# The values of differential attention made for two heads at a time, with x as the weights

## The chip, the cores and the metric

The kernel runs on one core of one Trainium2 chip. The metric is the device time of one execution in microseconds (us): lower is better. The engines are named as the profile names them: PE is TensorE (PEld its weight loads), DVE is VectorE, ACT is ScalarE, POOL is GpSimd, SP is the engine that issues the DMAs.

## What is computed

One step of a hybrid streaming encoder layer over 384 tokens: 256 of a prompt, and 16 new tokens of each of 8 sequences that have a cache of 128 earlier tokens. x has 2048 columns. One projection of x feeds two branches, differential attention (8 heads) and a gated delta rule (16 heads, "GDN" below). Their outputs are merged through gates, and a norm, cross attention and a feed-forward network follow. The part that matters here:

```python
def diff_attention_block(q, k, v, q_pos, k_pos, lam):
    s = jnp.einsum("bqhmd,bkhmd->bhmqk", q, k).astype(jnp.float32) * (DIFF_HEAD_DIM ** -0.5)
    ...
    p = jax.nn.softmax(jnp.where(allowed, s + bias, -jnp.inf), axis=-1)
    wts = p[:, :, 0] - lam * p[:, :, 1]
    return jnp.einsum("bhqk,bkhe->bqhe", wts.astype(v.dtype), v)
    ...
    proj = jnp.einsum("btd,de->bte", x, w_in)
    dq, dk, dv, gq, gk, gv, gz, ga, gb, gate_a, gate_b = split_in(proj)
    qd = dq.reshape(B, T, N_DIFF_HEADS, 2, DIFF_HEAD_DIM)
    kd = dk.reshape(B, T, N_DIFF_HEADS, 2, DIFF_HEAD_DIM)
    vd = dv.reshape(B, T, N_DIFF_HEADS, DIFF_VDIM)
    ...
    o_a = (rms_norm(o_a, diff_subln_g) * (1.0 - lam_init)).reshape(B, T, DIFF_WIDTH)
```

The keys and values of the new tokens are outputs of the kernel too (`dk`, `dv`).

## The kernel before

**Matrix jobs.** Every large product is a `Job` in one list that `stream` (line 400) works through. x and the weights are split in a high and a low part (`xh`, `xl`; `wh`, `wl`), and each product takes three fp32r matmuls: high by high, and twice high by low. Weights arrive in halves of 512 KB (8 tiles of 128 x 128) through four `raw` buffers. `prep` (line 376) casts a half to `wh` on ACT and subtracts on DVE to make `wl`; three pairs of such buffers run ahead of PE. There are two forms of job:

- `job` (line 341) uses the weights as the stationary operand and streams x's 384 tokens: 16 steps of 3 matmuls, 128 x 384, into one PSUM accumulator `acc`. The result has output channels on its partitions.
- `jobt` (line 358) uses tiles of 128 tokens of x as the stationary operand and streams 512 weight columns: 16 steps of 3 token tiles of 3 matmuls, 128 x 512, into three accumulators. The result has tokens on its partitions. Before the change it makes the cross attention's values from the memory (`memh`, `meml`), and the products of w_o (`mixh`), w_xo (`xoh`) and w_ff2 (`fh`).

The pool `psm` has three accumulators. A job's accumulator is emptied by a task of its own (`evac`).

**Attention.** `diff_jobs` (line 1163) makes for each head six such jobs of 128 channels: two of q, two of k, two of v. `begin` stands after head 0's six jobs; it closes the GDN branch and opens the attention's pools. From there `lane` takes the heads one after the other through `diff_head` (line 1266), a generator that runs between the matrix jobs. It first transposes v, 128 x 128 at a time, three into each of two PSUM tiles `dtr`, and ACT copies them to `vt`. Then come three query tiles: 0 (128 keys), 1 (256 keys), 2 (the new tokens, with the cache `kc`, `vc`). Each tile is one chain over the engines:

PE scores `dsc` -> DVE bias, maximum, scale (`dtt`, `dst`) -> ACT two exponentials with their sums -> DVE quotient and difference (`dtt`) -> PE transposes `dtr` -> ACT copy `dwT` (tile 2: DVE `dwz` too) -> PE product with the values `do` -> ACT squares `dsq` -> DVE `df` -> POOL power `df` -> ACT scaling `don` -> PE transposes into `do` -> DVE `doT`.

**Order.** The order on each engine is written out when the program is built. `Driver` keeps a rough clock for each engine. After each step of a job `poll` lets those tasks go on whose inputs are ready by that clock, so that a chain's next PE piece stands behind as many matrix matmuls as its wait seems to need. `until` is called where the stream must not go on before an event: it lets tasks run until the event is set, and no matrix matmul of a later job is issued meanwhile. On PE the attention's pieces and the matrix matmuls thus stand in one fixed row.

One such place is the start of a head's first q job (`job(h, 0, 0)`, `start`, line 1224): `if h > 1: d.until(done_ev[h - 2])`, so the q job of head h stands behind the whole of head h - 2. After the last head's jobs come 6 gate jobs, and then `merge_jobs` waits for the end of the attention (`opened`, line 1387).

Nearly all instructions are issued through one helper (`call`, line 117), and the profile gives them its line 118: they are told apart by their tiles.

Of the kernel before, what the change touches and what calls it, by code (L numbers as in the profile page):

```python
# [9 lines left out]
F32 = mybir.dt.float32  # L10
# [7 lines left out]
P = 128  # L18
D = 2048
KT = 16  # L20
# [302 lines left out]
class Kern:  # L323
# [33 lines left out]

    def jobt(self, w, lhs, nt, done, begin=None, ns=KT, mid=None, second=False, apart=0):


        halves = [(w, 8 * a, 8) for a in range(ns // 2)]
        if apart:
            halves = halves[:-apart] + [x + (i,) for i, x in enumerate(halves[-apart:])]
        cut = ns - 2 * apart
        order = [(k, t) for k in range(cut) for t in range(nt)] + [(k, t) for t in range(nt) for k in range(cut, ns)]
        quanta = [((k // 2, (k % 2, t), t, k, k == 0, k == ns - 1), lhs) for k, t in order]
        return Job(halves, quanta, nt, begin, done, GW, mid, second)
# [32 lines left out]
    def stream(self, jobs):  # L400
# [8 lines left out]
        for j in jobs:  # L409
# [5 lines left out]
            if not started:  # L415
                started = True
                d.spawn(self.prep(), prio=-1, lim=1e9)
            accs = []
            freed = freeds[j.second]
            for _ in range(j.nacc):  # L420
                if len(freed) >= 3:
                    d.until(freed[-3])
                freed.append(Ev())
                t = (self.psm2 if j.second else self.psm).tile([P, 512], F32, name="acc")
                accs.append(t[:, :j.n])
            last = {q[0]: i for i, (q, _) in enumerate(j.quanta)}
            for qi, ((hf, slot, ai, k, start, stop), rhs) in enumerate(j.quanta):
# [5 lines left out]
                if r[2] is not None:  # L433
                    d.until(r[2])
                d.until(h[:, 0:8], l[:, 0:8], r[0], r[1])
                acc = accs[ai]
                if isinstance(slot, tuple):
# [12 lines left out]
                if stop:  # L450
                    freed[len(freed) - j.nacc + ai] = j.done(ai, acc)
                d.poll()
# [710 lines left out]
    def diff_jobs(self):  # L1163
# [8 lines left out]
        self.b_ev = [Ev() for _ in range(KT)]  # L1172
        v_ev = [Ev() for _ in range(NDH)]
        done_ev = [Ev() for _ in range(NDH)]
# [21 lines left out]
        def lane():  # L1196
# [15 lines left out]
            for h in range(NDH):  # L1212
                heads[h]["kc"] = kc = s["at"].tile([P, 2, BS, P], F32, name="kc", bufs=1)
                d.sync.dma_start(out=kc, in_=I["cache_k"][h])
                heads[h]["vc"] = vc = s["at"].tile([P, BS, 256], F32, name="vc", bufs=1)
                d.sync.dma_start(out=vc, in_=I["cache_v"][h])
                yield tuple(evs[h, i] for i in range(6))
                yield from self.diff_head(h, heads[h], s, v_ev[h])
                done_ev[h].set()

        def job(h, i, m):
            e = evs[h, 2 * i + m] = Ev()

            def start():
                hd = heads[h]
                if i == 0 and m == 0:
                    if h > 1:
                        d.until(done_ev[h - 2])
                    if h == 0:
                        s["at0"] = d.pool(self.bctx, "at0", side="right")  # L1230
                    pool = s["at"] if h else s["at0"]
                    hd["q"] = pool.tile([P, 2, T], F32, name="dq")
                    hd["k"] = pool.tile([P, 2, T], F32, name="dk")
                    if h == 2:
# [4 lines left out]
                if i == 2 and m == 0:  # L1239
                    if h:  # L1240
                        d.until(v_ev[h - 1])
                    hd["v"] = s["at"].tile([P, 2, T], F32, name="dv", bufs=1) if h else s["at0"].tile([P, 2, T], F32, name="dv")

            def evac(acc):
                yield acc
                dst = heads[h]["qkv"[i]]
                d.scalar.copy(dst[:, m], acc)
                yield dst[:, m]
                if i:
                    d.sync.dma_start(out=self.O["dk" if i == 1 else "dv"][h * 2 + m], in_=dst[:, m])  # L1250
                e.set()

            return self.job(I["w_diff"][h * 6 + i * 2 + m], self.rx, lambda ai, acc: self.evl.spawn(evac(acc)), start)
# [12 lines left out]
    def diff_head(self, h, hd, s, v_ev):  # L1266
        nc, c = self.d, self.c
# [6 lines left out]
        for m in range(2):  # L1274
            sv = q[:, m, TP:].rearrange("p (g e t) -> p g e t", e=2, t=TS)
            dv = qz[m].rearrange("p (g e) (f t) -> p g e f t", e=2, t=TS)
            for e in range(2):
                nc.gpsimd.tensor_copy(dv[:, :, e, e], sv[:, :, e])
        vt = at.tile([P, 3, 256], F32, name="vt")
        for e in range(2):  # L1280
            ps = pstr.tile([P, 512], F32, name="dtr")
            yield ps[:], v[:, e]
            for t in range(3):
                nc.tensor.transpose(ps[:, t * P:(t + 1) * P], v[:, e, t * P:(t + 1) * P], ident)
            yield ps[:, 2 * P:T]
            nc.scalar.copy(vt[:, :, e * P:(e + 1) * P], ps[:, :T].rearrange("p (t d) -> p t d", d=P))
        v_ev.set()
        oT = at.tile([P, 2, T], F32, name="doT", bufs=1)
        for tile_ in (0, 1, 2):
# [40 lines left out]
            if tile_ < 2:  # L1330
                nc.scalar.copy(wT[:, :nk // P], ps[:, :nk].rearrange("p (j q) -> p j q", q=P))
                yield wT[:], o[:]
                for j in range(nk // P):
                    nc.tensor.matmul(o[:, :256], lhsT=wT[:, j], rhs=vt[:, j], start=(j == 0), stop=(j == nk // P - 1))
            else:
# [6 lines left out]
                yield wT[:], o[:], wzt[:], vc[:]  # L1342
                nc.tensor.matmul(o[:, :256], lhsT=wT[:, 1], rhs=vt[:, 2], start=True, stop=False)
                for e in range(2):
# [603 lines left out]
def pack(inp):  # L1948
# [35 lines left out]
    r["w_gate"] = np.concatenate([tiles(sec["gta"]), tiles(sec["gtb"])], axis=0)  # L1984
    hd = [tiles(sec[n]).reshape(NDH, 2, P, KT, P) for n in ("dq", "dk", "dv")]
    r["w_diff"] = np.stack(hd, axis=1).reshape(NDH * 6, P, KT, P)
    for nm in ("w_pa", "w_pb", "w_xq", "w_ff1", "w_ff3"):
        r[nm] = tiles(a[nm][0])
    wide = lambda w: w.reshape(-1, P, NG, GW).transpose(2, 1, 0, 3).reshape(NG, P, -1, P)
    r["w_o"] = wide(a["w_o"][0])  # L1990
    r["w_xo"] = wide(a["w_xo"][0])
# [19 lines left out]
    "dk": (2 * NDH, P, T),  # L2011
    "dv": (2 * NDH, P, T),
    "conv_p": (P, 48, 3),
# [8 lines left out]
def unpack(o):  # L2022
    c = np.ascontiguousarray
    y = o["y"].reshape(T, D)
    kv = [o[n].transpose(2, 0, 1).reshape(T, NDH, 256) for n in ("dk", "dv")]
    mem = [o["mk"].transpose(2, 0, 1).reshape(1, 1, NMEM, NXH, P), o["mv"].reshape(1, 1, NMEM, NXH, P)]
# [28 lines left out]
```

## Time and profile before

| | before |
|---|---|
| median of 3 runs (lowest, highest) | 3134.7 us (3133.63, 3136.52) |
| the profiled execution | 3136.02 us, of which 3133.8 us is the span of the trace |
| mean granted clock of TensorE | 0.989 |
| busy share of the span | PE 98%, PEld 93%, DVE 53%, ACT 37%, POOL 12% |
| HBM read, written | 450.78 MB, 38.50 MB |

The span is the time from the first to the last instruction; the execution has 2.2 us around it. Matmuls are pipelined and their ends are modelled, so what a matmul costs PE is the distance from its start to the next one's, not its own length. The attention occupies PE from 992 us to 1453 us.

### The profile page before, as it was taken

How to read it: one execution, taken by the hardware profiler on the slowest of the kernel's cores; microseconds unless marked ns; L12 is line 12 of the kernel's file. 1: busy time of each engine (PE TensorE's matmuls, PEld its weight loads, DVE VectorE, ACT ScalarE, POOL GpSimd, SP SyncE). 2: the span in 40 equal slices, each digit the busy share in tenths (PEclk: the TensorE clock that was granted, in tenths of full speed). 3: DMA queues.
4: the chain of work that ended last, by engine and by line, in shares of the span. 5: the costliest groups of instructions: out<-in, count | busy, mean ns of one | idle time of the engine just before them, and what ended most of it. 6: DMA issues, size and time to landing. Idle time of an engine off the chain costs nothing.

```text
span 3133.8 us, 46783 instructions
## 1 busy us (share of the span) xinstructions
PE 3069.3 (98%) x18059; PEld 2922.6 (93%) x18059; DVE 1661.9 (53%) x3470; ACT 1173.0 (37%) x2046; POOL 386.1 (12%) x638
## 2 busy tenths in 40 slices
PE   9999999999998999999999998899999999999997
PEld 8999999999998999999999777699999889999986
DVE  5476887788863444434344557843333333333335
ACT  5555555554432443333223224333322223223222
POOL 0344333443200000000000010000000000000001
PEclk9999999999999999999999998899999999999999
DMA  8455455554454564455444765333333433333443
GB/s 287 138 159 151 153 156 167 158 175 144 151 178 163 167 203 164 158 188 183 153 150 148 261 224 213 106 124 128 128 126 127 131 128 128 125 126 126 155 129 106
DMA packets 188640, 492.36 MB, mean 157 GB/s; under 512 B 42480, under 2 KB 78848, under 8 KB 183552
## 3 DMA queue, kind: packets, MB, share of 16 engines
q1 hardware_dynamic: 188416, 489.37, 47.4%
q8 instruction: 141, 2.31, 0.3%
q14 instruction: 83, 0.68, 0.1%
HBM read 450.78 MB, written 38.50 MB: 156 GB/s over the span
## 4 chain that ended last, share of the span: by engine, by line
PE 96%; DVE 2%; DMA 1%; issue 0%; ACT 0%; POOL 0%; SPq 0%; DVEq 0%; ACTq 0%
PE acc L118 90%; PE ch L118 1%; PE ps L118 1%; DVE R L118 1%; PE do L118 1%; PE o L118 1%; PE dsc L118 1%; PE fb L118 1%; DMA rawx<-in_memT 0%; PE dtr L118 0%; DVE hl L118 0%; DMA raw<-in_w_xo 0%; DMA xmk<-scr_mk 0%; PE xsp L118 0%; PE xss L118 0%
## 5 line engine op out<-in xcount | busy, mean ns | idle before, releaser
L118 DVE TENSOR_TENSOR wl<-raw,wh 128x1024 fp32r<-128x1024 f32 (+1 forms) x679 | 833.2, 1227 | 1016.9 <-ACT wh L118 1010.1
L118 ACT CAST wh<-raw 128x1024 fp32r<-128x1024 f32 (+1 forms) x679 | 711.9, 1049 | 1606.8 <-PE acc L118 1365.6
L118 PE MATMUL acc<-xh,wh 128*128 128x384 f32 x2320 | 817.2, 352 | 0.0
L118 PE MATMUL acc<-xh,wl 128*128 128x384 f32 x2320 | 779.8, 336 | 0.0
L118 PE MATMUL acc<-xl,wh 128*128 128x384 f32 x2320 | 778.6, 336 | 0.0
L118 PE MATMUL acc<-hl,wh 128*128 128x384 f32 x1472 | 494.9, 336 | 7.8 <-DVE hl L118 7.4
L118 PE MATMUL acc<-hh,wh 128*128 128x384 f32 x1472 | 497.1, 338 | 0.5 <-ACT hh L118 0.5
L118 PE MATMUL acc<-hh,wl 128*128 128x384 f32 x1472 | 493.8, 335 | 0.0
L118 PEld LDWEIGHTS acc<-xh,wh 128*128 128x128 f32 x2320 | 437.7, 189 | 9.9 <-issue 8.1
L118 PEld LDWEIGHTS acc<-xl,wh 128*128 128x128 f32 x2320 | 438.1, 189 | 1.5
L118 PEld LDWEIGHTS acc<-xh,wl 128*128 128x128 f32 x2320 | 436.7, 188 | 0.0
L118 PEld LDWEIGHTS acc<-hl,wh 128*128 128x128 f32 x1472 | 277.7, 189 | 11.1 <-DVE hl L118 10.8
L118 PEld LDWEIGHTS acc<-hh,wh 128*128 128x128 f32 x1472 | 277.7, 189 | 1.9 <-ACT hh L118 1.1
L118 PEld LDWEIGHTS acc<-hh,wl 128*128 128x128 f32 x1472 | 277.5, 189 | 0.0
L118 PE MATMUL acc<-wh,fl 128*128 128x512 f32 x498 | 194.0, 389 | 0.0
L118 PE MATMUL acc<-wl,fh 128*128 128x512 f32 x498 | 193.9, 389 | 0.0
L118 PE MATMUL acc<-wh,fh 128*128 128x512 f32 x498 | 193.9, 389 | 0.0
L118 POOL TENSOR_TENSOR cy<-cy,tap 128x408 f32<-128x408 f32 x144 | 174.1, 1209 | 67.8 <-ACT tap L118 58.1
L118 DVE SCALAR_TENSOR_TENSOR sol_u<-sol_mb,sol_u 128x31 f32<-128x31 f32 (+30 forms) x864 | 167.5, 269 | 0.0
L118 POOL TENSOR_TENSOR ln_mv<-ln_mv,mhalf 128x1 f32<-128x1 f32 x9 | 5.2, 581 | 1110.2 <-DVE ln_mv L118 1110.2
L118 PEld LDWEIGHTS acc<-wl,fh 128*128 128x128 f32 x498 | 93.5, 188 | 19.5
L118 PEld LDWEIGHTS acc<-wh,fl 128*128 128x128 f32 x498 | 93.5, 188 | 19.3
(288 smaller groups left out, 3608.7 us busy)
## 6 DMA issues: line engine op xcount, KB each, us to landing
raw<-in_w_ff SPq DMA_DIRECT2D x264, 512.0 KB
raw<-in_w_gdn SPq DMA_DIRECT2D x128, 512.0 KB
raw<-in_w_diff SPq DMA_DIRECT2D x96, 512.0 KB
raw<-in_w_gate SPq DMA_DIRECT2D x64, 512.0 KB
raw<-in_w_pb SPq DMA_DIRECT2D x32, 512.0 KB
raw<-in_w_pa SPq DMA_DIRECT2D x32, 512.0 KB
raw<-in_w_o SPq DMA_DIRECT2D x32, 512.0 KB
sol_ma<-scr_ma SPq DMA_DIRECT2D x8, 1024.0 KB
```

Source lines behind the costliest of these rows:

```text
L118: r = f(*a, **k)
```

## The change

v is no longer made per head with channels on the partitions. `vjob(p)`, a `jobt`, makes the values of heads 2p and 2p + 1 together: 3 token tiles, 512 columns. The weights are packed anew (`w_dv`), `diff_head` reads `v[:, j]` in place of `vt[:, j]`, and its six transposes and two copies are gone. The output `dv` is written by token tile.

The jobs' order is now: q and k of head 0; q of head 1; `begin`; values of heads 0 and 1; k of head 1; q and k of head 2; values of heads 2 and 3; q and k of head 3; q and k of head 4; values of heads 4 and 5; and so on. The wait on `done_ev[h - 2]` at the start of a head's first q job is as it was, and the values' job of pair p > 1 waits for head 2p - 3. `lane` starts a head when its q and k and all three tiles of its values are there. In `stream` an accumulator is now taken when its first matmul is issued, and `late` puts the third token tile's first two steps behind the others' first two.

```diff
-    def jobt(self, w, lhs, nt, done, begin=None, ns=KT, mid=None, second=False, apart=0):
+    def jobt(self, w, lhs, nt, done, begin=None, ns=KT, mid=None, second=False, apart=0, late=False):
...
+        if late:
+            order[:6] = [(0, 0), (0, 1), (1, 0), (1, 1), (0, 2), (1, 2)]
...
-            accs = []
+            accs, at = {}, {}
             freed = freeds[j.second]
-            for _ in range(j.nacc):
-                if len(freed) >= 3:
-                    d.until(freed[-3])
-                freed.append(Ev())
-                t = (self.psm2 if j.second else self.psm).tile([P, 512], F32, name="acc")
-                accs.append(t[:, :j.n])
...
+                if start:
+                    if len(freed) >= 3:
+                        d.until(freed[-3])
+                    at[ai] = len(freed)
+                    freed.append(Ev())
+                    accs[ai] = (self.psm2 if j.second else self.psm).tile([P, 512], F32, name="acc")[:, :j.n]
...
-                yield tuple(evs[h, i] for i in range(6))
-                yield from self.diff_head(h, heads[h], s, v_ev[h])
+                yield tuple(evs[h, i] for i in range(4)) + tuple(dv_ev[h // 2])
+                yield from self.diff_head(h, heads[h], s)
                 done_ev[h].set()
...
+        def vjob(p):
+            def start():
+                if p > 1:
+                    d.until(done_ev[2 * p - 3])
+                v = s["at"].tile([P, 3, GW], F32, name="dv")
+                for e in range(2):
+                    heads[2 * p + e]["v"] = v[:, :, 256 * e:256 * e + 256]
+                s["v", p] = v
...
+            def evac(t, acc):
+                yield acc
+                v = s["v", p][:, t]
+                d.scalar.copy(v, acc)
+                yield v
+                d.sync.dma_start(out=self.O["dv"][t][:, p * GW:(p + 1) * GW], in_=v)
...
+            return self.jobt(I["w_dv"][p], self.rx, 3, done, start, late=True)
 
         for h in range(NDH):
             if h == 1:
+                jobs.append(job(1, 0, 0))
+                jobs.append(job(1, 0, 1))
                 jobs.append(begin)
-            for i in range(3):
+                jobs.append(vjob(0))
+            for i in range(1 if h == 1 else 0, 2):
                 for m in range(2):
                     jobs.append(job(h, i, m))
+            if h and h % 2 == 0:
+                jobs.append(vjob(h // 2))
...
-        vt = at.tile([P, 3, 256], F32, name="vt")
-        for e in range(2):
-            ps = pstr.tile([P, 512], F32, name="dtr")
-            yield ps[:], v[:, e]
-            for t in range(3):
-                nc.tensor.transpose(ps[:, t * P:(t + 1) * P], v[:, e, t * P:(t + 1) * P], ident)
-            yield ps[:, 2 * P:T]
-            nc.scalar.copy(vt[:, :, e * P:(e + 1) * P], ps[:, :T].rearrange("p (t d) -> p t d", d=P))
-        v_ev.set()
...
-                    nc.tensor.matmul(o[:, :256], lhsT=wT[:, j], rhs=vt[:, j], start=(j == 0), stop=(j == nk // P - 1))
+                    nc.tensor.matmul(o[:, :256], lhsT=wT[:, j], rhs=v[:, j], start=(j == 0), stop=(j == nk // P - 1))
```

Three places show what becomes of the row of instructions on PE. The first is the start of the attention, right after `begin`: the difference of the two programs there (- before, + after). `acc` with 384 columns is a matrix job of the old form, with 512 columns one of the new, and `dtr<-cst_all,dv` are the transposes of v.

```order
 L118 MATMUL o_11462<-cst_all,y_11464 128x128 x3
-L118 MATMUL acc<-xh,wh 128x384
-L118 MATMUL acc<-xl,wh 128x384
-L118 MATMUL acc<-xh,wl 128x384
...
+L118 MATMUL acc<-wh,xh 128x512
+L118 MATMUL acc<-wl,xh 128x512
+L118 MATMUL acc<-wh,xl 128x512
...
 L118 MATMUL dtr<-lam,cst_all 128x2
...
-L118 MATMUL dtr<-cst_all,dv 128x128 x3
```

Head 0's work now stands behind the 144 matmuls of the first values' job, and its six transposes of v have gone.

The second place is the end of head 0's tile 1 and its whole tile 2 on PE. Before, each piece is followed by matrix matmuls: these are the rows from the last piece of tile 1 to the scores of tile 2 (`dqz` is the queries' layout for the cache), after which 36 `acc` matmuls stand.

```order
L118 MATMUL do<-cst_all,don 128x128 x2
L118 MATMUL acc<-xh,wh 128x384
L118 MATMUL acc<-xl,wh 128x384
L118 MATMUL acc<-xh,wl 128x384
L118 MATMUL dsc<-dk,dq 128x128 x2
L118 MATMUL dsc<-kc,dqz_11704 32x128 x8
L118 MATMUL dsc<-kc,dqz_11705 32x128 x8
L118 MATMUL acc<-xh,wh 128x384
```

In the change, six `acc` matmuls after the scores of tile 1, the rows are these:

```order
L118 MATMUL dtr<-cst_all,dtt 128x128 x2
L118 MATMUL do<-dv,dwT 128x256 x2
L118 MATMUL do<-cst_all,don 128x128 x2
L118 MATMUL dsc<-dk,dq_11058 128x128 x2
L118 MATMUL dsc<-kc,dqz_11702 32x128 x8
L118 MATMUL dsc<-kc,dqz_11703 32x128 x8
L118 MATMUL dtr<-cst_all,dtt 128x128 x2
L118 MATMUL do<-dv,dwT 128x256
L118 MATMUL do<-vc,dwz_11704 32x256 x8
L118 MATMUL do<-cst_all,don 128x128 x2
L118 MATMUL acc<-xh,wh 128x384
```

From the transposes of tile 1 to the end of tile 2 no matrix matmul stands between the pieces. The last row is the first of head 2's first q job. In heads 2 and 4 the end of tile 2, from its `dtr` to its last `do`, has the same gap-free form in front of the q jobs of heads 4 and 6, after 24 and 27 `acc` matmuls behind the scores; their other pieces are spread as before, and so are those of the odd heads and of head 6.

The third place is the end of the last head on PE, in the change:

```order
L118 MATMUL do<-dv,dwT 128x256
L118 MATMUL do<-vc,dwz_11705 32x256 x8
L118 MATMUL acc<-xh,wh 128x384
L118 MATMUL acc<-xl,wh 128x384
L118 MATMUL acc<-xh,wl 128x384
L118 MATMUL do<-cst_all,don 128x128 x2
L118 MATMUL acc<-bh,wh 128x384
```

Before, 24 `acc` matmuls stood between the product with the cached values and the last transposes; now 3 do, and the merge's first job (`bh`) follows at once.

## Rows read from the trace of the kernel before

**Rows 1.** The page's chain that ended last, over the whole span, by engine.

```profile
PE 96%; DVE 2%; DMA 1%; issue 0%; ACT 0%; POOL 0%; SPq 0%; DVEq 0%; ACTq 0%
```

**Rows 2.** That chain in one attention stretch: start us, us, engine, tile, count.

```profile
1141.23 0.86 PE do L118 x4
...
1147.02 1.45 PE dsc L118 x36
...
1154.94 0.22 PE dtr L118 x2
...
1157.27 1.43 PE do L118 x18
...
1163.61 0.22 PE do L118 x2
...
1170.62 0.33 PE dtr L118 x3
...
1190.21 0.86 PE dsc L118 x4
1191.07 6.25 PE acc L118 x36
```

**Rows 3.** Groups of PE instructions by shape: count | busy us, mean ns.

```profile
L118 PE MATMUL acc<-wl,mixh 128*128 128x512 f32 x192 | 75.9, 396 | 0.0
...
L118 PE MATMUL acc<-wl,memh 128*128 128x512 f32 x32 | 12.5, 390 | 0.0
...
L118 PE MATMUL dtr<-cst_all,dv 128*128 128x128 f32 x48 | 8.2, 282 | 0.0
```

**Rows 4.** Timeline, the first and last of 37 consecutive 512-column matmuls: start us, us.

```profile
2419.71 0.39 PE L118 MATMUL acc<-wl,fh 128*128 128x512 f32 x1
...
2427.87 0.39 PE L118 MATMUL acc<-wl,fh 128*128 128x512 f32 x1
```

**Rows 5.** Timeline of head 7's tile 1, its own instructions without the covering ones.

```profile
1421.62 1.03 PE L118 MATMUL dsc<-dk,dq 128*128 128x256 f32 x4
...
1425.91 0.48 DVE L118 SCALAR_TENSOR_TENSOR dtt<-dtt,dst 128x256 f32<-128x256 f32 x1
...
1428.73 0.38 PE L118 MATMUL dtr<-cst_all,dtt 128*128 128x128 f32 x2
...
1429.15 0.37 ACT L118 COPY dwT<-dtr 128x256 f32<-128x256 f32 x1 [0.47 <-PE dtr L118]
...
1430.54 1.02 PE L118 MATMUL do<-vt,dwT 128*128 128x256 f32 x4
...
1431.66 0.38 ACT L118 ACTIVATE dsq<-do 128x256 f32<-128x256 f32 x1 [2.14 <-PE do L118]
...
1432.40 0.54 POOL L118 TENSOR_TENSOR df<-df,mhalf 128x1 f32<-128x1 f32 x1 [16.18 <-DVE df L118]
...
1432.52 1.05 ACT L118 CAST wh<-raw 128x1024 fp32r<-128x1024 f32 x1 [0.39 <-ACT dsq L118]
...
1433.48 0.47 ACT L118 ACTIVATE don<-do,df 128x256 f32<-128x256 f32 x1
```

**Rows 6.** Timeline of head 6's tile 2, from the product with the values.

```profile
1388.68 0.59 PE L118 MATMUL do<-vt,dwT 128*128 128x256 f32 x2
...
1390.40 0.38 ACT L118 ACTIVATE dsq<-do 128x256 f32<-128x256 f32 x1 [3.36 <-PE do L118]
```

**Rows 7.** Timeline of PE where it waits for VectorE before head 0.

```profile
992.24 0.56 PE L118 MATMUL dtr<-lam,cst_all 128*128 128x2 f32 x2 [3.05 <-DVE lam L118]
```

**Rows 8.** Stretches: us, busy of five engines, PEclk, DMA share, GB/s.

```profile
982.00:988.00 6.00, 2.33 (x11) 1.94 (x10) 2.01 (x5) 0.88 (x6) 0.85 (x1) 0.69 0.48 153
...
995.00:998.00 3.00, 3.00 (x12) 3.00 (x11) 0.00 (x0) 0.48 (x1) 0.00 (x0) 0.51 1.01 410
998.00:1001.00 3.00, 3.00 (x20) 2.96 (x19) 0.89 (x1) 1.43 (x2) 0.00 (x0) 1.00 0.38 158
```

**Rows 9.** The same view, the stretch right after the attention.

```profile
1450.00:1500.00 50.00, 50.00 (x291) 49.97 (x290) 24.36 (x26) 19.59 (x23) 0.00 (x0) 1.00 0.69 224
```

More of the change, by code (lines that the diff above doesn't have):

```diff
@@ L450, in stream @@
                 if stop:
-                    freed[len(freed) - j.nacc + ai] = j.done(ai, acc)
+                    freed[at[ai]] = j.done(ai, acc)
                 d.poll()
@@ L1172, in diff_jobs @@
         self.b_ev = [Ev() for _ in range(KT)]
-        v_ev = [Ev() for _ in range(NDH)]
+        dv_ev = [[Ev() for _ in range(3)] for _ in range(NDH // 2)]
         done_ev = [Ev() for _ in range(NDH)]
@@ L1230, in start @@
                         s["at0"] = d.pool(self.bctx, "at0", side="right")
[L1231 to L1234, printed above, removed]
+                    hd["q"] = (s["at"] if h > 1 else s["at0"]).tile([P, 2, T], F32, name="dq%d" % (h == 1))
+                if i == 1 and m == 0:
+                    hd["k"] = (s["at"] if h else s["at0"]).tile([P, 2, T], F32, name="dk")
+                if h == 2 and i == 0 and m == 0:
                         def load():
@@ L1238, in start @@
                         ends.append(d.spawn(load(), prio=6))
[L1239 to L1242, printed above, removed]
             def evac(acc):
                 yield acc
-                dst = heads[h]["qkv"[i]]
+                dst = heads[h]["qk"[i]]
                 d.scalar.copy(dst[:, m], acc)
@@ L1249, in evac, with done @@
                 if i:
-                    d.sync.dma_start(out=self.O["dk" if i == 1 else "dv"][h * 2 + m], in_=dst[:, m])
+                    d.sync.dma_start(out=self.O["dk"][h * 2 + m], in_=dst[:, m])
                 e.set()
-            return self.job(I["w_diff"][h * 6 + i * 2 + m], self.rx, lambda ai, acc: self.evl.spawn(evac(acc)), start)
+            return self.job(I["w_diff"][h * 4 + i * 2 + m], self.rx, lambda ai, acc: self.evl.spawn(evac(acc)), start)
+        def vjob(p):
[6 more added lines that the diff above has]
+                s["v", p] = v
+            def done(t, acc):
+                return self.evl.spawn(evac(t, acc))
+            def evac(t, acc):
[4 more added lines that the diff above has]
+                d.sync.dma_start(out=self.O["dv"][t][:, p * GW:(p + 1) * GW], in_=v)
+                for e in range(2):
+                    x = heads[2 * p + e]["v"][:, t]
+                    d.ready[d.key(x)] = d.due(v)
+                dv_ev[p][t].set()
+            return self.jobt(I["w_dv"][p], self.rx, 3, done, start, late=True)
         for h in range(NDH):
             if h == 1:
+                jobs.append(job(1, 0, 0))
+                jobs.append(job(1, 0, 1))
                 jobs.append(begin)
-            for i in range(3):
+                jobs.append(vjob(0))
+            for i in range(1 if h == 1 else 0, 2):
                 for m in range(2):
                     jobs.append(job(h, i, m))
+            if h and h % 2 == 0:
+                jobs.append(vjob(h // 2))
         jobs += [self.gate_job(n) for n in self.gates]
@@ L1264, in diff_jobs, with diff_head @@
         return jobs
-    def diff_head(self, h, hd, s, v_ev):
+    def diff_head(self, h, hd, s):
         nc, c = self.d, self.c
@@ L1342, in diff_head @@
                 yield wT[:], o[:], wzt[:], vc[:]
-                nc.tensor.matmul(o[:, :256], lhsT=wT[:, 1], rhs=vt[:, 2], start=True, stop=False)
+                nc.tensor.matmul(o[:, :256], lhsT=wT[:, 1], rhs=v[:, 2], start=True, stop=False)
                 for e in range(2):
@@ L1984, in pack @@
     r["w_gate"] = np.concatenate([tiles(sec["gta"]), tiles(sec["gtb"])], axis=0)
-    hd = [tiles(sec[n]).reshape(NDH, 2, P, KT, P) for n in ("dq", "dk", "dv")]
-    r["w_diff"] = np.stack(hd, axis=1).reshape(NDH * 6, P, KT, P)
+    hd = [tiles(sec[n]).reshape(NDH, 2, P, KT, P) for n in ("dq", "dk")]
+    r["w_diff"] = np.stack(hd, axis=1).reshape(NDH * 4, P, KT, P)
     for nm in ("w_pa", "w_pb", "w_xq", "w_ff1", "w_ff3"):
@@ L2011 @@
     "dk": (2 * NDH, P, T),
-    "dv": (2 * NDH, P, T),
+    "dv": (3, P, D),
     "conv_p": (P, 48, 3),
@@ L2024, in unpack @@
     y = o["y"].reshape(T, D)
-    kv = [o[n].transpose(2, 0, 1).reshape(T, NDH, 256) for n in ("dk", "dv")]
+    kv = [o["dk"].transpose(2, 0, 1).reshape(T, NDH, 256), o["dv"].reshape(T, NDH, 256)]
     mem = [o["mk"].transpose(2, 0, 1).reshape(1, 1, NMEM, NXH, P), o["mv"].reshape(1, 1, NMEM, NXH, P)]
```

1 line of the change is left out of this document (added).

## The prediction

> **What bounds the kernel now.** I read the page's chain first: over the whole span 96% of it is PE [rows 1], so PE sets the time, and any other engine counts only where PE waits for it. Then the same chain inside the attention, in order of time. It goes from `acc` to an attention piece and back to `acc` with no wait between them: 36 matrix matmuls of 384 columns take 6.25 us, 0.1736 us each, and each attention piece shows what it costs PE while it is covered, 0.22 us for a pair of transposes up to 1.45 us for the scores of tile 2 [rows 2]. In this stretch PE is full; the chains of the attention over DVE, ACT and POOL are long but hidden, since enough matrix matmuls stand between their pieces. Last I read the timeline of two heads for the length of these chains without their cover [rows 5, 6]. So what PE no longer does is worth its price on PE, and what PE now waits for costs in full. Right after the attention PE is busy in all of 50 us at the full clock [rows 9]: there is no slack later that could take a loss back.
>
> **Gain 1, transposes.** 48 transposes of v go [rows 3], in 16 groups of three. A group costs PE 0.33 us [rows 2]: 16 x 0.33 = 5.3 us. Their 16 ACT copies and their waits go too; ACT does not bound here, so these are worth nothing by themselves, and neither are the 16 copies of v out of PSUM that become 12 longer ones. The DMAs of `dv` carry the same bytes in 12 issues for 16; none waits on the path.
>
> **Gain 2, the form of the job.** Per pair of heads v took 4 jobs of 48 matmuls: 192 x 0.1736 = 33.3 us. Now it takes 144 matmuls of 512 columns. The columns are the same (73728), so only the fixed part of each matmul can be saved. 37 matmuls of that form in the feed-forward part start over 8.16 us, 0.2267 us apart [rows 4]: 144 x 0.2267 = 32.6 us, a gain of 0.7 us a pair, 2.8 us in all. The bound on the other side: with `mixh` as weights one lasts 396 ns, with `memh` 390 [rows 3]; if x behaved like `mixh`, 0.2267 + 0.006 would give 33.5 us and turn 2.8 us of gain into 0.7 of loss. I take the first: in the program's memory map the tiles of x, `memh` and `fh` begin 32 bytes past a multiple of 128, and `mixh` 96 past one. That is all I find that tells the two groups apart, so both prices stay in the range. The Trainium skill ("TensorE: Matmul & The Clock Gate", section "Back-to-back issue gap") gives N/2.4 + 2.5 ns between matmuls: 162.5 and 215.8 ns, from which I would estimate a gain of only 0.5 us over the four pairs. The rows show a fixed part of some 13 ns in place of 2.5, and the measurement decides.
>
> The third accumulator of a values' job starts four steps late, about 2.7 us (12 x 0.2267), which covers the emptying of the job before it; at the job's end the first accumulator is complete six matmuls (1.4 us) ahead of the last. I cost both hand-overs at nothing; if that cover failed, it would be about 1 us of ACT cast [rows 5] a pair.
>
> **Loss 1, head 0.** The lane is no faster than before, but it starts later: head 0 must now wait for the whole first values' job, and only the two k jobs of head 1 (96 matmuls, 16.7 us) stand between that and the first q job of head 2, which the program puts behind the end of head 0. Before, the six jobs of head 1 (288 matmuls) stood in that place. The row of PE shows the result: after the scores of tile 1 only 6 matrix matmuls, then nothing but pieces of tiles 1 and 2. PE works in its row's order, so it idles through both chains.
>
> Tile 1 from its scores to the scaled output, from rows 5: scores to difference 1421.62 to 1426.39, 4.77 us; transposes to the end of the copy 1428.73 to 1429.52, 0.79; product to the end of the power 1430.54 to 1432.94, 2.40; scaling 0.47 (there held back by a weight cast, which does not stand there now). Three hand-overs to PE that the covered trace does not show I estimate at 0.2 us each (0.1 to 0.3). Sum 9.0 us. Tile 2: its scores cost PE 0.59 us more (1.45 for 0.86, rows 2), so 5.4 to the difference; 0.79; product to squares 1388.68 to 1390.40, 1.72 [rows 6]; squares to power 1.28 and scaling 0.47 as in tile 1; 0.6 for hand-overs: 10.3 us. With the last transposes of both (2 x 0.22) it is 19.7 us. Of this PE was to spend anyway 1.04 us (6 matmuls) and 5.5 us for the pieces (0.86 + 0.22 + 0.86 + 0.22 + 1.45 + 0.22 + 1.43 + 0.22, rows 2). Lost: 13.2 us.
>
> **Loss 2, heads 2 and 4.** Heads 4 and 6 wait for them in the same way, but there the four jobs of an odd head (192 matmuls) stand between, and only the end of tile 2 is bare: 0.79 + 0.2 + 1.72 + 1.28 + 0.47 + 0.2 + 0.22 = 4.9 us from `dtr` on, less 1.87 us of PE's own pieces, 3.0 us each. Head 2's chain has a weight subtraction and a split of the GDN's output on DVE in its way, so I add 0.5: 6.5 us for both. Head 6 has no q job behind it, and the odd heads are done long before theirs.
>
> **Loss 3, head 7.** Its last transposes stand 3 matrix matmuls behind the product for 24 before. On ACT a weight cast (1.05 us) and a gate's output stand ahead of the scaling, so 1.72 us to the squares, then some 2.5 to the scaled output and 0.2: 4.4 us, less 1.4 of the product and 0.5 of the three matmuls: 2.5 us.
>
> **Loss 4, the clock.** When GDN's end leaves PE little to do, busy 2.33 of 6 us, the granted clock falls to a mean of 0.69; dense matmuls go on from 992.2 us, run at half rate at 995 to 998 (0.51), and get 1.00 again from 998 [rows 7, 8]. That is 5 us of dense work at half rate, 2.5 us lost. Head 0's bare stretch is like it: 5.5 us of work in some 19. I add 2.5 us; the ends are 0 (the clock holds) and 4 (PE's own pieces inside the chain slow down too). The skill's same page (section "The HAM clock gate") says that the half rate is the default and activity releases it; rows 8 agree in both directions.
>
> **Sum.** -5.3 - 2.8 + 13.2 + 6.5 + 2.5 + 2.5 = +16.6 us. The profiled execution took 3136.0 us, 1.3 us over the median of 3134.7, so the new median is 3134.7 + 16.6 = 3151.3, rounded to 3151 us, 0.5% slower.
>
> **Rivals.** *PE does not wait.* If matmuls behind a waiting piece were run ahead of it, losses 1 to 4 would vanish: 3134.7 - 8.1 = 3126.6 us, faster by 0.26%. It decides from the point where more than 1.8 us of the 24.7 remain. Against it: PE stood still for 3.05 us at a `dtr` that waited for DVE though matrix matmuls stood behind it [rows 7]. The skill's page (section "What happens when you issue a matmul") says that only weight loads are pulled ahead and matmuls keep their order; row 7 agrees. 5%. *About no change (up to 3141).* The chains may be hidden better than the row suggests, if the bare chain is much shorter than its covered rows: at half of losses 1 to 3 and no loss of clock it is 3134.7 - 8.1 + 11.1 = 3137.7 us. For it: in the covered rows engines are shared with weight casts; against it: I took the pieces' own lengths already. 8%. *The clock stays low for longer*, and x as weights goes at the price of `mixh`. Four bare stretches could each cost 2.5 us as head 0's does, +7.5, and the form +3.5: 3162 us. For it: the 0.69 of rows 8 came with PE still busy for more than a third of the time; against it: three of the stretches are short, some 3 us of idleness. 17%. The forecast has the remaining 70%.
>
> **The numbers.** The forecast's own range is 3145 to 3158: hand-overs 1.2 either way, clock 0 to 4, the DVE work in heads 2 and 4. The range goes to 3143 below, toward the second rival, and 3161 above, toward the third. 0.2% (6.3 us) is about what a measurement of this kernel can tell from no change: faster 5%, same 8%, slower 87%.
>
> **What would show it.** In the new profile the groups `dtr<-cst_all,dv` and `vt` are gone and 576 matmuls `acc<-w..,x..` of 512 columns start some 0.227 us apart at 1.00. PE should show two bare tiles, together some 13 us idle, at the end of head 1's k jobs, some 50 us after the first values' job begins, with waits of DVE and ACT on `dsc` and `do` in the same stretch, and PEclk below 1.00 there or just behind; two waits of about 3 us, two heads apart; and one at the end of the gates. I would be wrong if PE's idle time in the attention stayed under 10 us, if x as weights cost over 0.23 us a matmul, or if the weights' buffers ran dry behind the stall: two halves (8 us) are ready there by the order of ACT and DVE.

## The result, and the profile after

| | before | changed |
|---|---|---|
| median (lowest, highest) | 3134.28 us (3133.63, 3136.52), 4 runs | 3156.7 us (3154.18, 3158.11), 4 runs |
| the profiled execution, its span | 3136.02, 3133.8 us | 3154.18, 3152.4 us |
| mean granted clock | 0.989 | 0.986 |

The changed kernel is slower: ratio 1.007, 95% interval 1.0056 to 1.0083, +22.4 us by the medians; the forecast was +16.6 us (3151, range 3143 to 3161). The whole loss is in the attention. From the first matrix matmul behind `dtr<-lam` to the first of the merge (`acc<-bh`) PE's row takes 485.6 us for 464.7, 20.9 more; what lies ahead of it and behind it took 1.2 and 1.1 us less. (The two profiled executions differ by 18.2 us only: before's lies 1.7 us over its median, the changed one's 2.5 under.) The page's chain is of little help here: followed back from the end it reaches 985 us and no further, and its shares are of the whole span:

```profile
PE 64%; DVE 2%; issue 1%; DMA 1%; ACT 0%; POOL 0%; SPq 0%; DVEq 0%; ACTq 0%; POOLq 0%
```

So I read stretches.

The stretches of the changed kernel, in the columns of [rows 8] (us, busy of PE, PEld, DVE, ACT and POOL, PEclk, DMA share, GB/s): the attention, the stretch right behind it, and six pieces of head 0's end.

```profile
992.00:1477.00 485.00, 464.39 (x2736) 423.17 (x2735) 195.84 (x346) 176.72 (x348) 20.23 (x57) 0.97 0.49 165
1480.00:1530.00 50.00, 50.00 (x290) 50.00 (x289) 25.22 (x26) 18.74 (x20) 0.00 (x0) 1.00 0.68 223
...
1042.00:1046.00 4.00, 1.42 (x8) 1.06 (x6) 3.01 (x6) 2.42 (x6) 0.00 (x0) 1.00 0.29 91
1046.00:1050.00 4.00, 2.73 (x6) 1.47 (x6) 0.75 (x3) 0.37 (x1) 0.00 (x0) 0.57 0.57 180
1050.00:1054.00 4.00, 2.04 (x19) 1.78 (x22) 0.58 (x2) 0.95 (x3) 0.55 (x1) 0.50 0.00 0
1054.00:1058.00 4.00, 1.37 (x28) 0.85 (x20) 1.54 (x3) 0.92 (x4) 0.00 (x0) 0.50 0.00 0
1058.00:1062.00 4.00, 2.35 (x12) 1.10 (x16) 1.35 (x6) 0.44 (x3) 0.00 (x0) 0.50 0.00 0
1062.00:1066.00 4.00, 2.03 (x21) 0.92 (x14) 0.24 (x2) 0.95 (x3) 1.25 (x5) 0.80 0.00 0
```

PE is idle for 20.6 of 485 us in the attention. Before, the same view shows 0.24 us of 461:

```profile
992.00:1453.00 461.00, 460.76 (x2956) 446.68 (x2957) 194.10 (x346) 179.93 (x366) 25.18 (x60) 0.99 0.50 171
```

The stretch behind it is as full as [rows 9], so nothing is given back. At head 0's end PE is busy for half of 24 us, and most of that half at the low clock level. The groups of PE show whose waits these are (busy us, mean ns | idle time before them, and what ended it); the group `dtr<-cst_all,dv` of [rows 3] is gone.

```profile
L118 PE MATMUL acc<-wh,xh 128*128 128x512 f32 x192 | 77.0, 401 | 0.0
L118 PE MATMUL do<-dv,dwT 128*128 128x256 f32 x64 | 19.6, 410 | 3.4 <-ACT dwT L118 3.4
L118 PE MATMUL do<-cst_all,don 128*128 128x128 f32 x48 | 10.0, 291 | 9.6 <-ACT don L118 9.6
L118 PE MATMUL dtr<-cst_all,dtt 128*128 128x128 f32 x40 | 8.8, 288 | 7.3 <-DVE dtt L118 3.9 <-DVE df L118 3.4
```

The chain through head 0's tiles 1 and 2 (start us, us, engine, tile, count). It is PE's own pieces and the waits between them, from the scores of tile 1 to the next matrix matmul:

```profile
1041.49 0.86 PE dsc L118 x4
1042.36 0.90 PE acc L118 x5
...
1043.28 1.04 ACT wh L118
1044.32 0.38 ACT dk L118
1044.70 1.00 ACT dtt L118 x4
...
1046.81 0.68 PE dtr L118 x2
...
1047.93 2.09 PE do L118 x4
...
1051.96 0.69 PE do L118 x2
1052.65 2.76 PE dsc L118 x36
...
1059.30 0.68 PE dtr L118 x2
...
1060.31 3.13 PE do L118 x18
...
1065.37 0.44 PE do L118 x2
1065.81 6.79 PE acc L118 x39
```

24.3 us from 1041.49 to 1065.81. The pieces from 1046.8 to 1063.4 take about twice their price in [rows 2], or more: 2.76 us for the scores of tile 2 where they took 1.45, 3.13 for the product where it took 1.43. The matrix matmuls behind it run at full speed at once (39 in 6.79 us).

Heads 2 and 4 have their bare ends too. Head 2's pieces on PE (timeline), with what ACT did ahead of the copy `dwT`, and the stretch right behind them:

```profile
1177.53 1.04 ACT L118 CAST wh<-raw 128x1024 fp32r<-128x1024 f32 x1 [1.46 <-issue]
1177.54 0.41 PE L118 MATMUL dtr<-cst_all,dtt 128*128 128x128 f32 x2
...
1178.48 0.47 ACT L118 COPY dk<-acc 128x384 f32<-128x384 f32 x1
...
1178.85 0.27 ACT L118 COPY dwT<-dtr 128x128 f32<-128x128 f32 x1
...
1179.17 0.70 PE L118 MATMUL do<-dv,dwT 128*128 128x256 f32 x2 [1.22 <-ACT dwT L118]
...
1180.02 1.07 PE L118 MATMUL do<-vc,dwz 128*32 128x256 f32 x16
...
1183.06 0.69 PE L118 MATMUL do<-cst_all,don 128*128 128x128 f32 x2 [1.97 <-ACT don L118]
```

```profile
1180.00:1183.00 3.00, 1.07 (x16) 0.42 (x16) 0.93 (x4) 1.46 (x4) 1.04 (x5) 1.00 0.58 156
1183.00:1186.00 3.00, 2.94 (x10) 2.94 (x11) 0.42 (x1) 0.14 (x2) 0.20 (x2) 0.51 0.70 257
1186.00:1189.00 3.00, 3.00 (x17) 3.00 (x17) 0.56 (x1) 0.38 (x1) 0.00 (x0) 0.92 1.04 308
```

The bare end lasts 6.2 us, from 1177.54 to the matrix matmul at 1183.75, and is over when the clock falls: 10 matmuls where the next stretch of that length has 17. Head 4 repeats it at 1296.67 to 1302.75. The chain shows the first matrix matmuls behind either end, 39 for the 39 behind head 0:

```profile
1183.75 8.11 PE acc L118 x39
...
1302.75 8.31 PE acc L118 x39
```

### The profile page after: what moved, and what is told of

It is laid out like the page before. It is cut to its first block, busy times and chain, and to the rows that moved or that the text cites. A ratio compares the mean times of both kernels' runs of the same rounds, so it can differ in the third digit from the quotient of the medians.

```text
span 3152.4 us, 46279 instructions
## 1 busy us (share of the span) xinstructions
PE 3069.6 (97%) x17819; PEld 2894.7 (92%) x17819; DVE 1661.0 (53%) x3470; ACT 1168.3 (37%) x2026; POOL 379.8 (12%) x638
## 4 chain that ended last, share of the span: by engine, by line
PE 64%; DVE 2%; issue 1%; DMA 1%; ACT 0%; POOL 0%; SPq 0%; DVEq 0%; ACTq 0%; POOLq 0%
PE acc L118 61%; PE do L118 1%; DVE R L118 1%; PE dsc L118 1%; PE fb L118 1%; DMA xmk<-scr_mk 0%; DVE hl L118 0%; PE xsp L118 0%; PE xss L118 0%; DMA raw<-in_w_xo 0%; DVE lu L118 0%; DVE fS L118 0%; PE dtr L118 0%; DVE ln_mv L118 0%; DVE wl L118 0%
## 5 line engine op out<-in xcount | busy, mean ns | idle before, releaser
L118 PE MATMUL acc<-xh,wh 128*128 128x384 f32 x2064 | 726.9, 352 | 0.0
L118 PE MATMUL acc<-xh,wl 128*128 128x384 f32 x2064 | 693.0, 336 | 0.0
L118 PE MATMUL acc<-xl,wh 128*128 128x384 f32 x2064 | 692.0, 335 | 0.0
L118 PEld LDWEIGHTS acc<-xh,wh 128*128 128x128 f32 x2064 | 389.4, 189 | 7.4 <-issue 5.4
L118 PEld LDWEIGHTS acc<-xl,wh 128*128 128x128 f32 x2064 | 389.7, 189 | 1.6
L118 PEld LDWEIGHTS acc<-xh,wl 128*128 128x128 f32 x2064 | 388.4, 188 | 0.0
L118 PEld LDWEIGHTS acc<-hl,wh 128*128 128x128 f32 x1472 | 277.0, 188 | 11.0 <-DVE hl L118 10.7
L118 PEld LDWEIGHTS acc<-wh,fh 128*128 128x128 f32 x498 | 93.5, 188 | 19.5
```

The lines of the kernel that those rows point to most:

```text
L118: r = f(*a, **k)
```

## The experiments

The theory (A below): the change's own work is cheaper on PE, and all that it loses is bare chains, in which PE waits for the lane of heads. The rivals put part of the loss or gain elsewhere. Ratios are to runs of the kernel before on the same chip (3134.7 to 3134.9 us), with 95% intervals.

**The wait of head 2's q job on head 0 taken away** (head 0's buffers come from a pool of their own, so that head 2 need not wait for them):

```diff
-                    if h > 1:
+                    if h > 2:
                         d.until(done_ev[h - 2])
```

> The changed kernel, but head 2's first q job no longer waits for the end of head 0 (h > 2 in place of h > 1). Theory A, the attention's lane has too little matrix work to hide in: the bare stretch is only passed on. By the order on PE head 0 is covered, the end of head 1's tile 2 becomes bare, head 2's tile 2 stands bare from 3 matrix matmuls behind its scores, and head 4 and head 7 stay as they were. From the changed kernel's trace: 17.8 us of head 0 go, the ends of tile 2 of heads 1 and 4 cost 5.7 us each, head 2 about 9, head 7 about 2, against 31.2 before: 3148 us, 3143 to 3153. Theory B, that one wait is the loss and nothing else needs the time: 3156.7 - 17.8 = 3139 us.

Measured: 3148.6 us (3146.1 to 3152.4), ratio 1.0045 (1.0033 to 1.0058). Head 0 is covered, but now the end of head 1's tile 2 is bare for 6.8 us before head 3's q job, and the ends of heads 2 and 4 stay bare (6.0 and 5.8 us up to the start of the next matrix matmul, 5.9 and 5.8 so counted in the changed kernel). Ahead of head 2's transposes PE now waits 3.8 us more. The wait was passed on: it was not this one wait that cost the time.

**Three buffers of queries, and waits one head later** (`dk` keeps two):

```diff
-                    if h > 1:
-                        d.until(done_ev[h - 2])
+                    if h > 4:
+                        d.until(done_ev[h - 3])
...
-                    hd["q"] = (s["at"] if h > 1 else s["at0"]).tile([P, 2, T], F32, name="dq%d" % (h == 1))
+                    hd["q"] = (s["at"].tile([P, 2, T], F32, name="dq", bufs=3) if h > 1 else s["at0"].tile([P, 2, T], F32, name="dq%d" % (h == 1)))
...
+                    if h > 2:
+                        d.until(done_ev[h - 2])
```

> The changed kernel with three buffers for q instead of two, so that a head's first q job waits for head h - 3 only (from head 5 on), and the wait for head h - 2 stands at its k job. Theory A: the lane of heads is still too slow for the matrix work that is left; by the order the ends of head 2's tile 2 (5.7 us) and of head 4 (about 2) stay bare, and the remainder collects at the last head, whose tile 2 stands bare as a whole before the merge (about 11): 3156.7 - 31.2 + 18.7 = 3144 us, 3139 to 3149. Theory B, the q jobs' waits are the loss: with all of them moved out of the way the gain stands alone, 3134.3 - 8.1 = 3126 us.

Measured: 3145.37 us (3144.32 to 3150.94), ratio 1.0037 (1.0024 to 1.005). Head 0 is covered, head 4 keeps one wait of 1.8 us, head 2's end is bare as in the changed kernel (5.8 us), and what the lane is behind comes out at the end of the attention: 12.9 us of head 7's tile 2 stand bare in front of the merge.

**Scores of tiles 0 and 1 start before the cached keys are loaded**; only tile 2 needs them:

```diff
-            yield sc[:], kc[:]
+            yield (sc[:], kc[:]) if tile_ == 2 else sc[:]
```

> The changed kernel, but tiles 0 and 1 of a head no longer wait for the cached keys, which only tile 2 reads: a head's scores can start right after the head before it. Theory A: the heads follow each other faster, head 7 gets its cover back (2 us), but the order still has head 0's bare stretch (17.8 us) and the ends of heads 2 and 4 (5.7 us each): 3154.5 us, 3150 to 3158. Theory C, the load of the cached keys is what keeps the lane behind everywhere: the bare stretches go, about 3128 us.

Measured: 3153.61 us (3151.35 to 3155.8), ratio 1.0061 (1.0048 to 1.0073). By the medians this is 3.1 us less than the changed kernel, but the runs of the two overlap, and PE's row takes 485.7 us in the attention for 485.6: a gain is not shown. Head 7's wait is gone, as expected; the other bare stretches stand at the same places, and the lane only waits longer for values (24.6, 24.6 and 31.4 us ahead of heads 2, 4 and 6, for 20.5).

**Both edits:**

> Both edits together: three buffers for q with the waits moved, and tiles 0 and 1 without the wait for the cached keys. By the order no attention piece is left without matrix matmuls around it. Theory A: what remains is the gain of the change, 5.3 us of transposes and 2.8 us of the job's form: 3134.3 - 8.1 = 3126 us, 3122 to 3130, faster than the kernel before. Theory D, values made with x as the weights cost more by themselves (hand-overs of three accumulators, weights from x, longer copies): 3134 us or more though nothing is bare.

Measured: 3125.05 us (3124.54 to 3125.9), ratio 0.9969 (0.9956 to 0.9981): faster than both kernels, by 31.6 us than the changed one, though alone the edits bring 11.3 us and 3.1 at most. Its attention, in the same columns, and the group that waited longest:

```profile
992.00:1449.00 457.00, 457.00 (x2740) 419.59 (x2740) 194.53 (x346) 174.68 (x347) 23.11 (x59) 0.99 0.53 175
```

```profile
L118 PE MATMUL do<-cst_all,don 128*128 128x128 f32 x48 | 9.1, 272 | 0.0
```

PE is never idle. By the medians the change's own work is then worth 9.7 us on the kernel before (by the ratio's interval 6 to 14). The traces say 7.8: PE's row takes 456.9 us in the attention for 464.7. Of the other 1.9 us, 0.5 lie ahead of it, where two jobs of v became two of q, and 1.4 behind it, where nothing was changed and the executions differ by up to 3 us.

**Control: the kernel before with the edit on the cached keys alone.**

> The kernel before, with the one edit that lets a head's scores of tiles 0 and 1 start before its cached keys are loaded. It is the control for the version in which nothing is bare. Theory A (in the kernel before nothing of the attention is bare, so a lane that gains a few us per head gains nothing in time, and the 9.7 us by which the change with both edits beats the kernel before are the change's own work saved on PE): 3134.7 us, within 1.5 us. Rival E (the earlier scores are worth something by themselves, whatever the values' jobs do): 3131 us or less, and the saving of the change proper is smaller by as much.

Measured: 3135.58 us (3133.91 to 3136.25), ratio 1.0 (0.9991 to 1.0009). Where nothing is bare, a lane that runs ahead is worth nothing that can be told (3 us either way by the interval; PE's row in the attention 463.8 us for 464.7). Three buffers of queries were not tried on the kernel before; that they too are worth nothing there is argued from PE's 0.24 us of idle time.

**The kernel before without its transposes of v:**

```diff
-        vt = at.tile([P, 3, 256], F32, name="vt")
-        for e in range(2):
...
+        vt = v.rearrange("p e t -> p (e t)").rearrange("p (t c) -> p t c", c=256)
```

The edit also gives `dv` a second buffer from head 1 on, because the product now reads it to the head's end.

> The kernel before without the transposes of v: the 48 transposes on PE and the 16 copies to vt are left out, and the product reads dv itself, rearranged, so that the attention's output is computed from values in the wrong layout; all else is as before, and nothing becomes bare by its row on PE. Theory T (the trace's 0.33 us for a covered group of three is what PE pays): 16 x 0.33 = 5.3 us less, 3129.4 us (3128 to 3131). Rival U (PE's small pieces are hidden by something else, the weights' buffers or the DMAs, so that taking them out gives nothing): 3134.7 us, within 2 us.

Measured: 3128.34 us (3126.32 to 3129.89), ratio 0.9979 (0.997 to 0.9988): 6.6 us less, 4 to 9 by the interval. That PE pays for transposes between matrix matmuls is confirmed, and 5.3 us lies in the interval. In the trace PE's row takes 458.3 us in the attention for 464.7, but 1.4 of these 6.4 us are the clock's: at 995 to 998 us it stood at 0.98, before at 0.51 [rows 8]. So 5.0 us are left for the transposes. The same stretch of this version, of the version with both edits and of the changed kernel:

```profile
995.00:998.00 3.00, 3.00 (x18) 3.00 (x18) 0.18 (x1) 1.05 (x1) 0.00 (x0) 0.98 1.03 421
995.00:998.00 3.00, 3.00 (x9) 2.33 (x8) 0.00 (x0) 0.37 (x1) 0.00 (x0) 0.55 0.97 404
995.00:998.00 3.00, 3.00 (x14) 2.45 (x13) 0.82 (x1) 1.05 (x1) 0.00 (x0) 0.94 1.01 421
```

**x moved to another place.** The version with both edits, with `xs.tile([P, 16], F32, name="xpad")` ahead of `xh`:

> The version with three buffers of queries and the freed scores, in which no stretch is bare (3125.05 us in the first call), with one change: 64 bytes of unused space in front of x in the memory of the core, so that x begins 96 bytes past a multiple of 128, as mixh does, in place of 32, as memh does. Theory P (the place is what makes mixh slower as weights than memh): the 512-column matmuls with x as weights start 0.233 us apart for 0.227, 576 x 0.006 = 3.5 us more, 3128.5 us (3127 to 3130); the 384-column ones, where x is streamed, stay at 0.1736. Rival Q (the place is irrelevant): 3125 us, within 1 us, and 0.227 as before.

Measured: 3126.8 us (3124.99 to 3129.58), ratio 0.9974 (0.9963 to 0.9985), 1.75 us more than without, just under the range of theory P; runs of either overlap. The trace decides. The groups of the version with both edits, then of this one:

```profile
L118 PE MATMUL acc<-wl,xh 128*128 128x512 f32 x192 | 76.3, 397 | 0.0
...
L118 PE MATMUL acc<-wl,memh 128*128 128x512 f32 x32 | 12.5, 389 | 0.0
```

```profile
L118 PE MATMUL acc<-wl,fh 128*128 128x512 f32 x498 | 193.8, 389 | 0.0
L118 PE MATMUL acc<-wl,xh 128*128 128x512 f32 x192 | 77.3, 403 | 0.0
...
L118 PE MATMUL acc<-wl,memh 128*128 128x512 f32 x32 | 12.7, 396 | 0.0
```

x and, moved along with it, `memh` become 6 to 7 ns longer; from start to start x goes from 0.227 to 0.233 us (medians over 192 matmuls); `fh`, which did not move, stays. **`mixh` and `mixl` moved the other way** (`mp.tile([P, 16], F32, name="mpad")` behind `mixl`):

> The version in which nothing is bare (3125.05 us), with 64 unused bytes behind the tiles of mixh and mixl, so that these two, the weights of the 576 matmuls of w_o, begin 32 bytes past a multiple of 128 in place of 96. It is the place of e4_shift turned round. Theory P (the place sets the price of tiles as weights): the matmuls with mixh and mixl start 0.227 us apart for 0.233, 576 x 0.006 = 3.5 us less, about 3121.5 us (3120 to 3123), and those with xoh, which stays at 96, keep 0.233. Rival Q: 3125 us, and 0.233.

Measured: 3121.31 us (3120.41 to 3121.78), ratio 0.9955 (0.9943 to 0.9968), the fastest of all. Its group, which answers to the first of [rows 3], and that of `xoh`, which was not moved:

```profile
L118 PE MATMUL acc<-wl,mixh 128*128 128x512 f32 x192 | 74.8, 390 | 0.0
...
L118 PE MATMUL acc<-wl,xoh 128*128 128x512 f32 x48 | 19.0, 395 | 0.0
```

396 became 390 ns, and 0.233 us from start to start 0.227. From the first to the last of the 576 matmuls it is 144.9 us for 148.3, 3.4 us less (3.7 by the medians). The place of the stationary tile sets this price.

**The clock in head 0's bare stretch.** The changed kernel with matmuls that nobody reads, to keep PE at work; `keep` issues n of 128 x 256 into unused columns of `dtr`, for head 0's tiles 1 and 2. First 30 right behind the scores, 4 behind the transposes and 15 behind the product:

> The changed kernel, with matmuls whose results nobody reads put into head 0's tiles 1 and 2 (30, 4 and 15 of 128 x 256 at the three waits of each tile, into unused columns of dtr) so that PE stays busy in the bare stretch. Theory A (the granted clock fell to half inside the chain, and the pieces that the chain waits for took twice as long there): the clock stays at 1.00 between 1046 and 1064, the pieces take about half as long, and the stretch from the scores of tile 1 shrinks by 3.9 us: about 3153 us (3151 to 3155). Rival C (the chain's length is set by DVE, ACT and POOL alone, and PE's half clock cost it nothing): 3156.7 us or more, by what the added matmuls delay a piece (up to 3 us: 3160).

Measured: 3158.01 us (3151.46 to 3159.32), ratio 1.007 (1.0057 to 1.0082). By its number the rival has it, but the trace shows a flaw of the experiment: the 30 stood ahead of matrix matmuls whose weights' buffer ACT was waiting for, so ACT's cast and with it the exponentials came 3.6 us later (cast at 1046.88 for 1043.28 us). PE was idle meanwhile, and the clock did not hold either (0.53 at 1050 to 1054). Tile 2, which had no such cast, went from 13.2 us (scores to the next matrix matmul) to 10.7, with the clock at 1.00 from 1058 on. So a second try, behind the matrix matmuls:

```diff
+            if warm:
+                keep(ps, 28)
             for j in range(nk // P):
                 nc.tensor.transpose(ps[:, j * P:(j + 1) * P], w[:, j * P:(j + 1) * P], ident)
+            if warm:
+                keep(ps, 4)
...
+            if warm:
+                keep(ps, 11)
```

> The changed kernel with unread matmuls in head 0's tiles 1 and 2 again, but now behind the matrix matmuls and right ahead of the transposes (28, then 4 behind them and 11 behind the product), so that they cannot hold up the cast of weights on ACT as the 30 of e7_keep did. Theory A (half clock inside the chain makes the pieces that it waits for twice as long): clock 1.00 from 1043 to 1064 and, over the two tiles, about 0.35 us less for each of two pairs of transposes, 1.0 for the product of tile 1, 1.2 for the scores of tile 2, 1.4 for its product and 0.5 for the last transposes: 4.8 us less, about 3152 us (3150 to 3154). Rival C (the clock costs the chain nothing that counts): 3156.7 us, within 1 us.

Measured: 3152.16 us (3149.67 to 3153.45), ratio 1.0053 (1.004 to 1.0065), 4.5 us less than the changed kernel. One of its stretches, and two pieces of its chain:

```profile
1050.00:1054.00 4.00, 3.35 (x51) 2.83 (x50) 1.24 (x3) 0.47 (x1) 0.55 (x1) 1.00 0.00 0
```

```profile
1051.63 1.50 PE dsc L118 x36
...
1062.30 1.74 PE acc L118 x10
```

The clock holds at 1.00, the scores of tile 2 take 1.50 us for 2.76, and the stretch from tile 1's scores ends at 1062.30 for 1065.81: 3.5 us of the 24.3 were the low clock inside the chain.

**The version with both edits, without the late third accumulator** (`late=False`):

> The version in which nothing is bare (3125.05 us), without the part of the change that lets the third accumulator of a values' job start four steps late. Theory H (the late start hides the emptying of the job before it): each of four values' jobs waits about 1 us at its start for an accumulator, 3129 us (3127.5 to 3130). Rival I (an accumulator is free in time anyway, or the wait is taken up by the pieces that stand there): 3125 us, within 1 us.

Measured: 3126.43 us (3124.39 to 3128.96), ratio 0.9972 (0.9963 to 0.9982); 1.4 us more, with overlapping runs. In the trace the attention ends at the same time to 0.1 us, and no values' job waits more than 0.2 us at its start. The emptying is covered without the late start as well.

## Why the prediction was right, and where its terms were off

The direction, the mechanism and the places came as said. The sum was 5.8 us short, because the losses were costed too low: by 6.6 us if the terms below are added up.

| term | predicted | measured | from |
|---|---|---|---|
| gains 1 and 2 | -8.1 | -7.8; by medians -9.7 (6 to 14) | version with both edits against before |
| hand-overs of accumulators | 0 | 0 | trace with and without the late start |
| loss 1, head 0 without the clock | 13.2 | 14.3 | 24.3 - 1.04 - 5.5 - 3.5 |
| loss 4, clock at head 0 | 2.5 | 3.5 | stretch of the second run with unread matmuls |
| loss 2, heads 2 and 4 | 6.5 | 11.4 | below |
| loss 3, head 7 | 2.5 | 2.1 | wait of 1.92 ahead of the last `do`, and its 0.44 for 0.22 us |
| losses 1 to 4 | 24.7 | 31.3 | sum; by medians 3156.7 - 3125.05 = 31.6, by the traces' attention 485.6 - 456.9 = 28.7 |

That the terms add up to the medians' 31.6 us is partly luck: they are read from one execution, whose attention lost only 28.7 us. About 1.2 us of the difference is the low clock at the attention's start, which cost the version with both edits more (0.55 for 0.94 at 995 to 998). About 0.8 us more is the covered price of two pieces. From matmul to matmul the timeline has tile 2's scores and its product at 1.65 and 1.63 us, where the chain in [rows 2] gives 1.45 and 1.43, so PE was to spend 0.4 us more anyway at head 0 and 0.2 each at heads 2 and 4. The remaining 0.6 us is open.

**Gains.** Both terms stand: the transposes by their own experiment, the form by 0.227 us from start to start, as [rows 4]. In the traces 7.8 us less the 5.0 of the transposes leave 2.8 for the form, as predicted. The Trainium skill ("TensorE: Matmul & The Clock Gate", section "Back-to-back issue gap") has a fixed 2.5 ns in the gap of a matmul taken by itself; by that I estimate 0.5 us for the form. x as weights shows 227 ns from start to start, some 13 over the 213.3 of 512 columns at 2.4 GHz, so the measurement decides again. That `memh` and `mixh` are told apart by their place, on which the form's term rested, is shown.

**Loss 1 and loss 4.** Tile 1 took 10.5 us to its scaled output reaching PE for 9.0 predicted, tile 2 12.7 for 10.3. Most of the difference is PE's own pieces at half clock: the far end of my bound for the clock ("PE's own pieces inside the chain slow down too", 4 us), not the 2.5 that I took, which I had placed behind the stretch, after the likeness of [rows 8]. Behind it the clock was back at once, in this execution. About 0.6 us more is the weight cast (1.04 us) and the copy of `dk` (0.38), which ACT did ahead of tile 1's exponentials (their input was there at 1044.01 us, they began at 1044.60): I had read the chain's lengths from rows where another cast stood in another place.

**Loss 2** is the term that was mis-sized. The bare ends last 6.2 and 6.1 us, less 1.87 of PE's own pieces 4.3 and 4.2, where I had 3.0 each and 0.5 for both. In both heads the copy `dwT` stood behind a cast and a copy of `dk` on ACT and began 1.3 and 1.4 us after the transposes, where [rows 5] have 0.4: some 0.9 us each that I had read from another order of jobs. And I had no clock term for them; the first 39 matrix matmuls behind the ends took 8.1 and 8.3 us, where those behind head 0 took 6.79: 1.3 and 1.5 us more. In all 11.4 us. The third rival had this mechanism ("the clock stays low for longer", 2.5 us at each of three more stretches); in this execution it came at two of them and at half its price, without its other half, the price of `mixh`.

**Rivals.** PE did wait, 20.6 us. What the prediction named as its undoing did not occur: x costs 0.227 us, and behind the stall 39 matmuls ran in 6.79 us, so no weights were missing.

**What the prediction did not see** is why four places wait at once. With values for two heads the lane and the stream wait for each other in turn. After head 1 the lane stands still: its last transposes on PE at 1121.06, the scores of head 2 at 1141.63 us, and between them PE works at the second values' job, which the lane needs whole. 36 us after these scores, at 1177.54, PE has no matrix matmul left ahead of the q job of head 4, which needs head 2 done. Before, the lane's pause between two heads was never over 10.2 us by the same two pieces. So taking away one wait moved it (first experiment), more room let the lag reach the end (second), a faster lane only paused longer (third), and only room and speed together removed all of it, though even then the lane pauses for 12.3 and 16.4 us ahead of heads 4 and 6.

## What to carry to other kernels

When an edit makes a job coarser, follow both who must wait for the whole of it and who waits for them: work saved on the full engine (8 to 10 us) is lost three times over where the row leaves a chain bare, and then one wait taken away only shows the next. Cost a bare chain with the engine's own pieces at the lower clock, and look at what other engines do ahead of it in the new order, not in the old rows. When two groups of one shape have different means, look at where their stationary tiles begin: one unused tile of 64 bytes was worth 3.4 us.

## What the hardware showed that I had not expected

- The place of a stationary fp32r tile changes the time of a 512-column matmul: 0.227 us from start to start for tiles that begin 32 bytes past a multiple of 128, 0.233 for 96 (the places by the program's memory map; the traces do not print them). A move by 64 bytes made x and `memh` slower and `mixh` and `mixl` faster, and tiles that did not move kept their price. Other places were not tried, and why it is so stays open.
- The clock falls at different times. In the changed kernel's trace it fell inside head 0's stretch (0.57 at 1046 to 1050, 0.50 from there on), but only as the bare ends of heads 2 and 4 were over (1.00 at 1180 to 1183, 0.51 at 1183 to 1186), so that dense work paid for idleness that was past. Around head 7's wait of 1.9 us it did not fall (1.00 at 1474 to 1480). 86 unread matmuls held it at 1.00 in head 0.
- The same places can come out otherwise in another execution. With the 86 unread matmuls the clock stayed up behind head 2's bare end but fell right behind the same wait of head 7 (first two lines below), and with the scores freed alone it stayed low for 5 us of matrix matmuls behind head 0's stretch (third line). So what the clock costs at one place is known for one execution only.

```profile
1179.00:1183.00 4.00, 3.46 (x21) 3.46 (x22) 0.98 (x2) 0.99 (x2) 0.69 (x4) 1.00 0.85 289
1473.00:1476.00 3.00, 3.00 (x11) 3.00 (x10) 0.00 (x0) 0.00 (x0) 0.00 (x0) 0.51 0.83 205
...
1068.00:1073.00 5.00, 5.00 (x19) 5.00 (x18) 2.18 (x7) 0.88 (x4) 0.00 (x0) 0.50 0.73 220
```
